# Hybrid decoder layer on one core: block sums on DVE straight from PSUM, norm sums five products later, a third buffer of decays, the gates' tanh as a job

## Chip, cores and metric

One core of a Trainium2 chip runs the whole layer in one launch. The metric is the device time of a launch in microseconds (us), the median of several runs.

## What is computed

One layer of a decoder trunk on 1024 tokens of width 1024, float32. One wide projection feeds three mixers, and their outputs are gated, summed, projected and normalised:

```python
h = rms_norm(x, g_pre)
proj = jnp.einsum('bsd,dc->bsc', h, w_in)
(q, k, v, z_a, u, v_s, z_s, z_m, xbc, dt_raw, gate_logits) = jnp.split(proj, _split_points(), axis=-1)
y_att = sliding_window_attention(q, k, v, sinks, rel_bias) * jax.nn.silu(z_a)
y_sg = chunked_spatial_gate(u, v_s, sg_ln_g, sg_ln_b, sg_w, sg_b) * jax.nn.silu(z_s)
y_ssm = ssd_mixer(z_m, xbc, dt_raw, conv_w, conv_b, dt_bias, a_log, d_skip, ssm_norm_g)
gates = jax.nn.sigmoid(gate_logits.reshape(bsz, seq, N_BRANCHES, D_MODEL))
merged = (gates[:, :, 0] * (y_att @ w_br_att) + gates[:, :, 1] * (y_sg @ w_br_sg)
          + gates[:, :, 2] * (y_ssm @ w_br_ssm))
out = merged @ w_out
return x + rms_norm(out, g_post)
```

`ssd_mixer` (Mamba-2) takes a causal convolution over four tokens and a silu of `xbc`, then scans 8 chunks of 128 tokens in each of 4 groups of 8 heads. A chunk needs the decays `exp(a_cs[l] - a_cs[s])`, a product within the chunk, a product with the carried state, a new state, the skip term, the product with `silu(z)`, and the sum of squares for a norm over the group.

## The kernel before

**Engines and queues.** Each engine works through its own instructions in the order in which they were written, and waits for semaphores of the others: TensorE (PE) for matmuls, VectorE (DVE), ScalarE (ACT) and GpSimd (POOL) for elementwise work, SyncE (SP) for all DMAs. The stage that the change is in has its order written out by hand for all five.

**Products.** That stage computes the projections for xBC, z_m, z_s and u, and most of the gates by a seven-product scheme for 2x2 blocks (Strassen's in Winograd's form). A *unit* is a pair of 128-column tiles of w_in; 39 units make 273 *products*. `PairStream._step` issues one product: it prepares weights up to four products ahead (`_prepare`: POOL block sums in `_sum`, an ACT cast `whi`, and one product later a DVE subtraction `wlo`, L230, in `_second`), then issues 12 matmuls into one of four PSUM banks (three of `ps_mm`, one of `ps_ax`; L290 to L292), and then the sums that make the four output blocks 11, 12, 21 and 22 out of the seven products, in tiles `tp` (8 buffers) and `tu`.

**Block sums before.** Product 0 is copied out by ACT (`s1`, L308), product 1 added by DVE (`u2`, L311). Product 2 is copied out by ACT (`s5`, L313), and POOL adds it to `u2` (`u4`, L314). Product 3 is added by DVE (`u3`, L316), and POOL adds `s5` and `u3` to block 22 (L304). Products 4, 5 and 6 are added by DVE (L302) and end blocks 12, 21 and 11.

**Jobs.** What follows on a block is a generator that is put in `pst.waiting`: a convolution (`conv`: three L781 taps on DVE, a tanh on ACT, L788 on DVE, a store), a silu (`z_pair`, `zu_pair`). `_work`, the last thing that `_step` does, advances two of them by a step, four when the queue is long. A gate's tanh and its store (L725, L727) stand in `gate_pair`'s own `evac`, at once behind the block.

**Chunks.** While products run, the scan of the 32 chunks goes on between them. `chunk(n)` is a generator too; the loop at the end of the stage advances each running chunk by one step ahead of each product, and begins one every 6 products (5 in the last group). In it: the score matmul and the transposes (L873 to L877), two halves of decays (`seg`, filled by a broadcast load; `relu` and an exp on ACT, `local` on DVE, L867), the state product `po` (L912) read by DVE into `t1` (L914), the new state `pn` (L917), the chunk's own product `pd` (L927), added to `y` by DVE (L931), `t1` added by POOL (L933), the product with silu(z) on POOL (L938), its square on ACT (L943), two POOL sums over the square (L945, L946), and, one step behind the sums, a matmul with a column of ones that adds over the partitions (L949). `po`, `pn` and `pd` share two PSUM banks (`ps_a2`), so that `pd` is written where `po` stood.

Ahead of this stage lie attention and the first projections; behind it the spatial gate's mixing (`sg_mix`, between the last products), then the four branch projections and the output.

Of the kernel before, what the change touches and what calls it, by code (L numbers as in the profile page):

```python
# [19 lines left out]
P = 128  # L20
# [19 lines left out]
def hybrid_kernel(ctx, tc, t, out):  # L40
# [153 lines left out]

    class PairStream:
        AHEAD = 4

        def __init__(self, pool, lhs):
            self.pool, self.lhs = pool, lhs
            self.units, self.raw, self.b, self.ops, self.slot = [], {}, {}, {}, None  # L200
            self.prepared = self.done = 0
            self.late = None
            self.waiting, self.active, self.begun = [], [], []
# [57 lines left out]
        def _work(self):  # L261

            for _ in range(2 if len(self.waiting) > 3 else 1):
# [7 lines left out]
        def _step(self):  # L271
# [27 lines left out]
            def block(b, eng, name, x, op=ALU.add):  # L299
                d = t[name][:, 4:]  # L300
                if x is o:
                    eng.tensor_tensor(d, d, o, op=op)  # L302
                else:
                    eng.tensor_tensor(d, x, d, op=op)  # L304
                self.units[u][1](b, t[name])

            if i == 0:
# [4 lines left out]
            elif i == 2:  # L312
                A.copy(tmp("s5"), o)  # L313
                G.tensor_tensor(tmp("u4"), t["u2"], t["s5"][:, 4:], op=ALU.add)  # L314
            elif i == 3:
                V.tensor_tensor(tmp("u3"), t["u2"], o, op=ALU.add)  # L316
                block(22, G, "s5", t["u3"][:, 4:])
            elif i == 4:
                block(12, V, "u4", o)
            elif i == 5:  # L320
                block(21, V, "u3", o, ALU.subtract)
            else:
                block(11, V, "s1", o)
            self._work()
# [412 lines left out]
    def z_pair(g, n):  # L737
# [7 lines left out]
        def evac(b, d):  # L745
            pst.waiting.append(silu(b, d[:, 4:]))
        return [t["w_zm"][2 * g + n][k] for k in range(2)], evac

    def zu_pair(g):
# [11 lines left out]
        def evac(b, d):  # L761
# [4 lines left out]
            else:  # L766
                pst.waiting.append(silu(half, d, us.pop(half)))
        return [t["w_zu"][g][k] for k in range(2)], evac

    def conv_pair(g, n):  # L770
# [23 lines left out]
        def evac(b, d):  # L794
# [7 lines left out]
            pst.waiting += [conv(0, k, d), conv(1, k, d1)]  # L802
# [17 lines left out]
    with tc.tile_pool(name="mp", bufs=1, reuse_waits="tile") as mp, tc.manual_schedule(  # L820
# [18 lines left out]
        def load_a(n):  # L839
            g, c = divmod(n, 8)  # L840
            rows = acs_dr[c * 32 + g * 8:c * 32 + g * 8 + 8, :]
            segs[n] = []
            for i in range(2):
                seg = mp.tile([P, 4, P], F32, name="seg", bufs=2)
                src = rows[i * 4:(i + 1) * 4].rearrange("h l -> (h l)").unsqueeze(0).broadcast_to([P, 4 * P])
                nc.sync.dma_start(out=seg.rearrange("p h l -> p (h l)"), in_=src)
                segs[n].append(seg)
            if c > 0:

                eas[n] = mp.tile([P, 4, P], F32, name="ea")  # L850
                for i in range(2):
                    src = rows.rearrange("(j i) l -> i j l", i=2)[i].unsqueeze(0).broadcast_to([64, 4, P])
                    nc.sync.dma_start(out=eas[n][i * 64:(i + 1) * 64], in_=src)

        def chunk(n):

            g, c = divmod(n, 8)
            seg = segs[n]

            def relu(i):  # L860

                for j in range(4):
                    A.activation(seg[i][:, j, :], seg[i][:, j, :], AF.Relu, scale=-1.0,
                                 bias=acs[:, c, g * 8 + i * 4 + j:g * 8 + i * 4 + j + 1])

            def local(i):
                V.tensor_tensor(seg[i], seg[i], gt.unsqueeze(1).broadcast_to([P, 4, P]), op=ALU.mult)  # L867
# [39 lines left out]
            local(1)  # L907
            if c > 0:
# [4 lines left out]
                t1 = mp.tile([P, 4, P], F32, name="t1")  # L913
                V.scalar_tensor_tensor(t1, v4(po), 0.5, eas.pop(n), op0=ALU.mult, op1=ALU.mult)  # L914
# [10 lines left out]
            for h in range(8):  # L925
                r = slice((h % 2) * 64, (h % 2) * 64 + 64)
                T.matmul(pd[r, (h // 2) * P:(h // 2 + 1) * P], lhsT=xd[:, h * 64:(h + 1) * 64],  # L927
                         rhs=seg[h // 4][:, h % 4, :], start=True, stop=True)
# [5 lines left out]
            if c + 1 < NB:  # L934
                load_a(n + 1)
            yield

            G.tensor_tensor(y, y, zz.pop(n), op=ALU.mult)  # L938
            yield
            if c + 1 < NB:  # L940
                load_z(n + 1)
            sq = mp.tile([P, 4, P], F32, name="t1")
            A.activation(sq, y, AF.Square)  # L943
            yield
            G.tensor_tensor(sq[:, 0:2, :], sq[:, 0:2, :], sq[:, 2:4, :], op=ALU.add)  # L945
            G.tensor_tensor(sq[:, 0, :], sq[:, 0, :], sq[:, 1, :], op=ALU.add)  # L946
# [4 lines left out]
            for j in range(4):  # L951
                A.activation(y[:, j, :], y[:, j, :], AF.Copy, scale=ng[:, g * 4 + j:g * 4 + j + 1])
            if g < 3:
                yield
# [278 lines left out]
```

## Time and profile before

| | |
|---|---|
| median of 3 runs | 1933.63 us (1925.47 to 1934.16) |
| the profiled execution | 1927.05 us, its span 1925.2 us |
| mean granted TensorE clock | 0.966 of full speed |
| the stage with the products | 425 to 1450 us of the span |

The profile is of one execution. Busy time is the time in which an engine executed an instruction; PEld is the load of weights into TensorE. The granted clock of TensorE is 1.00 at 2.4 GHz and 0.50 at 1.2 GHz; a mean between lies over both.

### The profile page before, as it was taken

How to read it: one execution, taken by the hardware profiler on the slowest of the kernel's cores; microseconds unless marked ns; L12 is line 12 of the kernel's file. 1: busy time of each engine (PE TensorE's matmuls, PEld its weight loads, DVE VectorE, ACT ScalarE, POOL GpSimd, SP SyncE). 2: the span in 40 equal slices, each digit the busy share in tenths (PEclk: the TensorE clock that was granted, in tenths of full speed). 3: DMA queues.
4: the chain of work that ended last, by engine and by line, in shares of the span. 5: the costliest groups of instructions: out<-in, count | busy, mean ns of one | idle time of the engine just before them, and what ended most of it. 6: DMA issues, size and time to landing. Idle time of an engine off the chain costs nothing. (4 is left out here: it accounts for less than half of the span.)

```text
span 1925.2 us, 26009 instructions
## 1 busy us (share of the span) xinstructions
PE 1784.2 (93%) x9181; PEld 1493.1 (78%) x9181; DVE 1297.5 (67%) x1815; ACT 838.5 (44%) x1938; POOL 848.9 (44%) x759
## 2 busy tenths in 40 slices
PE   7999999989998889888988998997996999999998
PEld 6988888968886767666866776776884888888898
DVE  6466676578988976898598856776876453535423
ACT  5245555434455565655565556562223120212221
POOL 1026666564546755666565655676545300000000
PEclk9999999989998989999999999998997999999999
DMA  6211111213344544444454444443566453533204
GB/s 222 93 45 44 56 44 56 75 58 94 106 142 135 159 147 129 151 141 137 144 159 121 139 150 143 148 143 116 194 197 242 170 186 98 176 109 109 96 26 154
DMA packets 165378, 243.29 MB, mean 126 GB/s; under 512 B 13152, under 2 KB 105600, under 8 KB 165120
## 3 DMA queue, kind: packets, MB, share of 16 engines
q1 hardware_dynamic: 165248, 241.63, 39.2%
q8 instruction: 73, 1.20, 0.3%
q14 instruction: 57, 0.47, 0.1%
HBM read 177.99 MB, written 63.59 MB: 125 GB/s over the span
## 5 line engine op out<-in xcount | busy, mean ns | idle before, releaser
L115 PE MATMUL ps_mm<-y,whi 128*128 128x512 f32 x512 | 201.9, 394 | 9.8 <-ACT y L1061 9.8
L116 PE MATMUL ps_mm<-y,whi 128*128 128x512 f32 x512 | 202.2, 395 | 7.2 <-DVE y L1062 7.2
L290 PE MATMUL ps_mm<-h,whi 128*128 128x512 f32 x468 | 200.2, 428 | 4.8 <-ACT vst L354 2.8
L117 PE MATMUL ps_mm<-y,wlo 128*128 128x512 f32 x512 | 201.4, 393 | 0.0
L292 PE MATMUL ps_mm<-h,wlo 128*128 128x512 f32 x468 | 188.2, 402 | 5.7 <-DVE wlo L230 5.7
L225 POOL TENSOR_TENSOR ts<-ts,raw 128x512 f32<-128x512 f32 x78 | 124.4, 1594 | 149.0 <-DVE wlo L230 119.3
L291 PE MATMUL ps_mm<-h,whi 128*128 128x512 f32 x468 | 188.6, 403 | 0.0
L97 ACT CAST whi<-raw 128x1024 fp32r<-128x1024 f32 (+1 forms) x69 | 71.6, 1039 | 255.9 <-PE ps_mm L116 227.5
L88 POOL TENSOR_TENSOR rso<-rso,mhalf_row 128x1 f32<-128x1 f32 x8 | 4.4, 554 | 402.3 <-DVE rso L87 402.3
L230 DVE TENSOR_TENSOR wlo<-raw,whi 128x512 fp32r<-128x512 f32 x156 | 158.2, 1015 | 6.9 <-ACT whi L255 6.4
L290 PE MATMUL ps_mm<-S,whi 128*128 128x512 f32 x352 | 148.9, 423 | 0.0
L291 PE MATMUL ps_mm<-S,whi 128*128 128x512 f32 x352 | 141.7, 402 | 0.0
L292 PE MATMUL ps_mm<-S,wlo 128*128 128x512 f32 x352 | 141.3, 401 | 0.0
L781 DVE SCALAR_TENSOR_TENSOR acc<-tp,wcv,acc 128x512 f32<-128x512 f32 x144 | 137.6, 982 | 1.7
L230 DVE TENSOR_TENSOR wlo<-ts,whi 128x512 fp32r<-128x512 f32 x117 | 105.9, 906 | 26.9 <-ACT whi L255 26.8
L1084 DVE SCALAR_TENSOR_TENSOR tm<-gld,ps_mm 128x512 f32<-128x512 f32 x48 | 33.0, 687 | 135.1 <-PE ps_mm L117 135.1
L115 PEld LDWEIGHTS ps_mm<-y,whi 128*128 128x128 f32 x512 | 97.5, 190 | 31.6 <-ACT y L1061 11.1
L115 PE MATMUL ps_mm<-h,whi 128*128 128x512 f32 x304 | 120.9, 398 | 0.1
L116 PEld LDWEIGHTS ps_mm<-y,whi 128*128 128x128 f32 x512 | 97.4, 190 | 30.4 <-DVE y L1062 10.5
L117 PE MATMUL ps_mm<-h,wlo 128*128 128x512 f32 x304 | 118.6, 390 | 0.0
L116 PE MATMUL ps_mm<-h,whi 128*128 128x512 f32 x304 | 118.5, 390 | 0.0
L290 PEld LDWEIGHTS ps_mm<-h,whi 128*128 128x128 f32 x468 | 92.1, 197 | 29.4 <-issue 8.4
(239 smaller groups left out, 4982.2 us busy)
## 6 DMA issues: line engine op xcount, KB each, us to landing
seg<-acs_dr SPq DMA_DIRECT2D x64, 256.0 KB, 3.8
raw<-in_w_br_dram SPq DMA_DIRECT2D x32, 512.0 KB, 4.3
yraw<-y_dr SPq DMA_DIRECT2D x32, 512.0 KB, 4.7
gld<-gate_dr SPq DMA_DIRECT2D x32, 512.0 KB, 3.5
raw<-in_w_xbc_dram SPq DMA_DIRECT2D x24, 512.0 KB, 4.0
raw<-in_w_gp_dram SPq DMA_DIRECT2D x22, 512.0 KB, 3.6
gate_dr<-tp SPq DMA_DIRECT2D x44, 256.0 KB, 2.5
raw<-in_w_zm_dram SPq DMA_DIRECT2D x16, 512.0 KB, 3.5
```

The source lines that it names most:

```text
L88: G.tensor_tensor(dst, dst, mhalf, op=ALU.pow)
L97: A.copy(hi, raw)
L115: T.matmul(ps, lhsT=whi[:, ks], rhs=rhs(0, kt, half), start=kt == 0, stop=False)
L116: T.matmul(ps, lhsT=whi[:, ks], rhs=rhs(1, kt, half), start=False, stop=False)
L117: T.matmul(ps, lhsT=wlo[:, ks], rhs=rhs(0, kt, half), start=False, stop=kt == KT - 1)
L225: G.tensor_tensor(b[out], b[x], b[y], op=op)
L230: V.tensor_tensor(lo, src, hi.bitcast(F32), op=ALU.subtract)
L290: T.matmul(o, lhsT=hi[:, ks], rhs=h0, start=kt == 0, stop=False)
L291: T.matmul(o, lhsT=hi[:, ks], rhs=h1, start=False, stop=False)
L292: T.matmul(o, lhsT=lo[:, ks], rhs=h0, start=False, stop=kt == 3)
L781: V.scalar_tensor_tensor(acc, d[:, 1 + tap:513 + tap], wcv[:, ti, tap:tap + 1], acc, op0=ALU.mult, op1=ALU.add)
L1084: V.scalar_tensor_tensor(tm, gt[0][:, fs], 1.0, ps, op0=ALU.add, op1=ALU.mult)
```

## The change

- **Block sums.** `u4` is made by DVE, by adding product 2 straight from PSUM to `u2`; block 22 (`c22`) is made by DVE, by adding product 3 from PSUM to `u4`. The ACT copy `s5` and both POOL sums are gone. Per unit: one ACT instruction and two POOL instructions less, two DVE instructions more.
- **Order in `_step`.** `_work` stands ahead of the product's block sums, and new jobs go to a list `fresh`, which `_work` takes up one product later. The gates' tanh is such a job.
- **Chunks.** A chunk begins two products later. The first half of its decays is loaded one chunk ahead, with three buffers instead of two, and its relu is issued in the chunk before. `local` comes one product earlier. `t1` takes the place of `ea`, so that the load of the next `ea` waits for POOL's sum. The square goes into the tile of silu(z) and comes one product later, the load of the next silu(z) behind the POOL sums; their result has a tile of its own, `ssy`. The matmul over the partitions comes three products behind the POOL sums, and with the later start five products later than before.
- **Tail.** Two products run between the first `sg_load` and the mixing; jobs left over are finished behind the last product.

```diff
@@ PairStream._work, _step
+            self.waiting, self.fresh = self.waiting + self.fresh, []
...
-            def block(b, eng, name, x, op=ALU.add):
+            def block(b, name, op=ALU.add):
                 d = t[name][:, 4:]
-                if x is o:
-                    eng.tensor_tensor(d, d, o, op=op)
-                else:
-                    eng.tensor_tensor(d, x, d, op=op)
+                V.tensor_tensor(d, d, o, op=op)
                 self.units[u][1](b, t[name])
 
+            self._work()
             if i == 0:
                 A.copy(tmp("s1"), o)
             elif i == 1:
                 t["u2"] = self.pool.tile([P, 512], F32, name="tu", bufs=1)
                 V.tensor_tensor(t["u2"], t["s1"][:, 4:], o, op=ALU.add)
             elif i == 2:
-                A.copy(tmp("s5"), o)
-                G.tensor_tensor(tmp("u4"), t["u2"], t["s5"][:, 4:], op=ALU.add)
+                V.tensor_tensor(tmp("u4"), t["u2"], o, op=ALU.add)
             elif i == 3:
+                V.tensor_tensor(tmp("c22"), t["u4"][:, 4:], o, op=ALU.add)
                 V.tensor_tensor(tmp("u3"), t["u2"], o, op=ALU.add)
-                block(22, G, "s5", t["u3"][:, 4:])
+                self.units[u][1](22, t["c22"])
...
-            self._work()
             return 2.8
@@ gate_pair
-        def evac(b, d):
-            d = d[:, 4:]
+        def tanh(b, d):
             A.activation(d, d, AF.Tanh, scale=0.5)
...
+            yield from ()
+
+        def evac(b, d):
+            pst.fresh.append(tanh(b, d[:, 4:]))
@@ loads and chunk(n)
+        def load_a(n, i):
+            seg = mp.tile([P, 4, P], F32, name="seg", bufs=3)
...
+            A.activation(segs[n, 0], segs[n, 0], AF.Exp, scale=-1.0)
+            if c + 1 < NB:
+                load_a(n + 1, 0)
             yield
...
-            relu(0)
+            local(0)
+            relu(n, 1)
             yield
 
-            A.activation(seg[0], seg[0], AF.Exp, scale=-1.0)
-            relu(1)
-            yield
-
-            local(0)
-            A.activation(seg[1], seg[1], AF.Exp, scale=-1.0)
+            A.activation(segs[n, 1], segs[n, 1], AF.Exp, scale=-1.0)
             if c > 0:
                 A.activation(eas[n], eas[n], AF.Exp)
+            yield
+
+            if c == 0:
+                load_z(n)
+            local(1)
             if g < 3:
                 yield
 
-            local(1)
             if c > 0:
...
-                t1 = mp.tile([P, 4, P], F32, name="t1")
-                V.scalar_tensor_tensor(t1, v4(po), 0.5, eas.pop(n), op0=ALU.mult, op1=ALU.mult)
+                t1 = eas.pop(n)
+                V.scalar_tensor_tensor(t1, v4(po), 0.5, t1, op0=ALU.mult, op1=ALU.mult)
...
             if c + 1 < NB:
-                load_a(n + 1)
+                load_a(n + 1, 1)
+                relu(n + 1, 0)
             yield
 
-            G.tensor_tensor(y, y, zz.pop(n), op=ALU.mult)
+            if c + 1 < NB:
+                load_e(n + 1)
+            sq = zz.pop(n)
+            G.tensor_tensor(y, y, sq, op=ALU.mult)
             yield
+            yield
+            A.activation(sq, y, AF.Square)
...
+            yield
+            ss = mp.tile([P, P], F32, name="ssy")
+            G.tensor_tensor(sq[:, 0:2, :], sq[:, 0:2, :], sq[:, 2:4, :], op=ALU.add)
+            G.tensor_tensor(ss, sq[:, 0, :], sq[:, 1, :], op=ALU.add)
             if c + 1 < NB:
                 load_z(n + 1)
...
             yield
+            nc.sync.dma_start(out=y_dr[g * 4:(g + 1) * 4, :, c * P:(c + 1) * P].rearrange("j p s -> p j s"), in_=y)
+            yield
             yield
             pn = psum(ps_tr, "tr")
-            T.matmul(pn[:, 0:1], lhsT=sq[:, 0, :], rhs=one, start=True, stop=True)
+            T.matmul(pn[:, 0:1], lhsT=ss, rhs=one, start=True, stop=True)
@@ the loop, the mixing, the tail
-                begin[46 + 49 * g + (6 if g < 3 else 5) * c] = g * 8 + c
+                begin[48 + 49 * g + (6 if g < 3 else 5) * c] = g * 8 + c
...
         sg_load(0)
+        pst.run(2)
+        left -= 2
...
     pst.run(4)
+    while pst.fresh or pst.waiting or pst.active:
+        pst._work()
```

What the change moves in the written order is seen at three places. The first is PE at the end of a product, where before the matmul over the partitions (L949) stands alone, ahead of the next product:

```order
L290 MATMUL ps_mm<-S_4294,whi 128x512
L291 MATMUL ps_mm<-S_4295,whi 128x512
L292 MATMUL ps_mm<-S_4294,wlo 128x512
L949 MATMUL ps_tr<-mhalf_row,t_7997 128x1
L290 MATMUL ps_mm<-h_111,whi 128x512
```

Now it is L965, reads `ssy`, and stands ahead of the transposes of a chunk that begins two chunks later:

```order
L294 MATMUL ps_mm<-h_109,wlo 128x512
L965 MATMUL ps_tr<-mhalf_row,ssy 128x1
L876 MATMUL ps_tr<-bcch 128x128
L877 MATMUL ps_tr<-ident,bcch 128x128
L880 MATMUL ps_tr<-ident,xch 128x128 x4
L292 MATMUL ps_mm<-S_4294,whi 128x512
```

The matmul moved; PE's other work stays, with new line numbers. The second place is POOL over the same chunk; before, from the product with silu(z) (L938) to the norm sums (L945, L946), which stand behind two weight sums (L225), the block sums `u4` (L314) and 22 (L304), and the scaling of `xdt` (L892):

```order
L938 TENSOR_TENSOR y<-y,zch 128x512
L225 TENSOR_TENSOR ts<-raw 128x512
L314 TENSOR_TENSOR tp<-tu,tp 128x512
L892 TENSOR_TENSOR xde<-xdt,edec 128x512
L225 TENSOR_TENSOR ts<-ts,raw 128x512
L304 TENSOR_TENSOR tp<-tp 128x512
L945 TENSOR_TENSOR t_7997<-t_7997 128x256
L946 TENSOR_TENSOR t_7997<-t_7997 128x128
```

And now, from the same product (L948) to the sums (L956, L957):

```order
L948 TENSOR_TENSOR y<-y,zch 128x512
L226 TENSOR_TENSOR ts<-raw 128x512
L898 TENSOR_TENSOR xde<-xdt,edec 128x512
L226 TENSOR_TENSOR ts<-ts,raw 128x512
L226 TENSOR_TENSOR raw<-raw 128x512
L956 TENSOR_TENSOR zch<-zch 128x256
L957 TENSOR_TENSOR ssy<-zch 128x128
```

The two block sums went. The third place is DVE around the read of `po` (L914), in a unit whose convolution runs; before, with the taps (L781) behind the block sums (L302) of the product:

```order
L230 TENSOR_TENSOR wlo<-raw,whi 128x512
L302 TENSOR_TENSOR tp<-tp,ps_mm 128x512
L788 SCALAR_TENSOR_TENSOR tp<-tp,acc 128x512 x2
L867 TENSOR_TENSOR seg<-seg,gtm 128x512
L914 SCALAR_TENSOR_TENSOR t_7880<-ps_ac,ea 128x512
L230 TENSOR_TENSOR wlo<-ts,whi 128x512
```

And now, where the read is L920, the silu of a job L744, and the new block sums from PSUM L313 (`u4`) and L315 (block 22):

```order
L231 TENSOR_TENSOR wlo<-raw,whi 128x512
L744 SCALAR_TENSOR_TENSOR tp<-acc,tp 128x512 x2
L311 TENSOR_TENSOR tu<-tp,ps_mm 128x512
L920 SCALAR_TENSOR_TENSOR ea<-ps_ac,ea 128x512
L231 TENSOR_TENSOR wlo<-ts,whi 128x512
L313 TENSOR_TENSOR tp<-tu,ps_ax 128x512
L936 TENSOR_TENSOR st<-st,ps_ac 128x512
L937 TENSOR_TENSOR y<-y,ps_ac 128x512
L231 TENSOR_TENSOR wlo<-raw,whi 128x512
L744 SCALAR_TENSOR_TENSOR tp<-acc,tp 128x512 x2
L315 TENSOR_TENSOR tp<-tp,ps_mm 128x512
L316 TENSOR_TENSOR tp<-tu,ps_mm 128x512
```

A product's job steps stand ahead of its block sum, the second half of the decays no longer stands between the block sum and the read of `po`, and two sums per unit are new.

## Rows read from the trace of the kernel before

**Rows 1.** Busy us of each engine over the span, instructions (the page).

```profile
PE 1784.2 (93%) x9181; PEld 1493.1 (78%) x9181; DVE 1297.5 (67%) x1815; ACT 838.5 (44%) x1938; POOL 848.9 (44%) x759
```

**Rows 2.** Waits of PE: line, waited for, us in total, times, longest.

```profile
PE ps_tr L949 <- POOL t L946: 63.3, 26, 4.1
PE ps_ac L927 <- DVE t L914: 10.7, 6, 2.5
...
PE ps_tr L977 <- POOL ssum L974: 6.5, 1, 6.5
```

**Rows 3.** Stretches: us, busy PE, PEld, DVE, ACT, POOL, then clock, DMA.

```profile
436.00:550.00 114.00, 114.00 (x505) 94.39 (x504) 101.49 (x139) 51.64 (x89) 57.51 (x36) 1.00 0.34 104
425.00:1450.00 1025.00, 931.65 (x4499) 749.81 (x4499) 808.29 (x1080) 531.28 (x1216) 608.92 (x430) 0.95 0.46 143
786.20:984.20 198.00, 175.24 (x858) 139.48 (x858) 159.90 (x214) 114.40 (x271) 120.21 (x86) 0.95 0.46 143
1165.00:1329.00 164.00, 146.39 (x735) 116.20 (x735) 116.15 (x154) 86.18 (x218) 112.75 (x82) 0.94 0.41 130
1329.00:1450.00 121.00, 118.35 (x577) 99.25 (x576) 94.84 (x122) 35.37 (x62) 63.64 (x44) 0.97 0.62 201
813.70:816.90 3.20, 3.20 (x9) 2.53 (x8) 0.00 (x0) 2.71 (x7) 0.07 (x1) 0.50 0.27 82
```

**Rows 4.** Timeline of POOL ahead of one wait of PE: start, us, what.

```profile
803.90 1.74 POOL L314 TENSOR_TENSOR tp<-tu,tp 128x512 f32<-128x512 f32 x1
805.60 1.50 POOL L892 TENSOR_TENSOR xde<-xdt,edec 128x512 f32<-128x512 f32 x1
807.06 1.73 POOL L225 TENSOR_TENSOR ts<-ts,raw 128x512 f32<-128x512 f32 x1
808.75 1.72 POOL L304 TENSOR_TENSOR tp<-tp 128x512 f32<-128x512 f32 x1
810.43 1.24 POOL L945 TENSOR_TENSOR t<-t 128x256 f32<-128x256 f32 x1
811.75 0.78 POOL L946 TENSOR_TENSOR t<-t 128x128 f32<-128x128 f32 x1
```

**Rows 5.** The wait on PE, in the timeline: start, us, [idle before].

```profile
812.59 0.38 PE L949 MATMUL ps_tr<-mhalf_row,t 128*128 128x1 f32 x2 [4.08 <-POOL t L946]
```

**Rows 6.** DVE groups from 786.2 to 984.2: busy us, mean ns, idle before.

```profile
L781 DVE SCALAR_TENSOR_TENSOR acc<-tp,wcv,acc 128x512 f32<-128x512 f32 x36 | 34.9, 996 | 0.4
L230 DVE TENSOR_TENSOR wlo<-raw,whi 128x512 fp32r<-128x512 f32 x28 | 28.0, 1001 | 0.4 <-ACT whi L255 0.3
L230 DVE TENSOR_TENSOR wlo<-ts,whi 128x512 fp32r<-128x512 f32 x21 | 19.6, 933 | 6.1 <-ACT whi L255 6.1
L867 DVE TENSOR_TENSOR seg<-seg,gtm 128x512 f32<-128x512 f32 x16 | 14.2, 889 | 2.1 <-ACT seg L901 1.8 <-ACT seg L896 0.4
L788 DVE SCALAR_TENSOR_TENSOR tp<-tp,acc 128x512 f32<-128x512 f32 x12 | 12.8, 1105 | 0.0
L742 DVE SCALAR_TENSOR_TENSOR tp<-acc,tp 128x512 f32<-128x512 f32 x8 | 10.9, 1397 | 0.0
```

**Rows 7.** Three DVE lines over the run: ns least/median/most, first and last start.

```profile
L302 DVE TENSOR_TENSOR tp<-tp,ps_mm x88: 672/680/690, 445.0 to 1451.4; 128x512 f32<-128x512 f32 x88
...
L781 DVE SCALAR_TENSOR_TENSOR acc<-tp,wcv,acc x144: 737/747/1789, 448.3 to 1103.0; 128x512 f32<-128x512 f32 x144
...
L742 DVE SCALAR_TENSOR_TENSOR tp<-acc,tp x32: 675/942/1792, 473.8 to 1060.8; 128x512 f32<-128x512 f32 x32
```

**Rows 8.** POOL groups from 786.2 to 984.2.

```profile
L304 POOL TENSOR_TENSOR tp<-tp 128x512 f32<-128x512 f32 x7 | 11.5, 1650 | 2.0 <-issue 1.3 <-POOL ts L225 0.7
...
L314 POOL TENSOR_TENSOR tp<-tu,tp 128x512 f32<-128x512 f32 x7 | 10.0, 1435 | 7.4 <-ACT tp L313 7.1 <-ACT ssum L950 0.3
```

**Rows 9.** Waits of DVE from 786.2 to 984.2, the three that are named.

```profile
DVE wlo L230 <- ACT whi L255: 6.4, 4, 4.5
...
DVE seg L867 <- ACT seg L901: 1.8, 2, 1.4
...
DVE seg L867 <- ACT seg L896: 0.4, 1, 0.4
```

More of the change, by code (lines that the diff above doesn't have):

```diff
@@ L202, in __init__ @@
             self.late = None
-            self.waiting, self.active, self.begun = [], [], []
+            self.fresh, self.waiting, self.active, self.begun = [], [], [], []
         def add(self, *units):
@@ L745, in evac @@
         def evac(b, d):
-            pst.waiting.append(silu(b, d[:, 4:]))
+            pst.fresh.append(silu(b, d[:, 4:]))
         return [t["w_zm"][2 * g + n][k] for k in range(2)], evac
@@ L766, in evac @@
             else:
-                pst.waiting.append(silu(half, d, us.pop(half)))
+                pst.fresh.append(silu(half, d, us.pop(half)))
         return [t["w_zu"][g][k] for k in range(2)], evac
@@ L801, in evac @@
             V.tensor_copy(d1[:, 1:4], d[:, 513:516])
-            pst.waiting += [conv(0, k, d), conv(1, k, d1)]
+            pst.fresh += [conv(0, k, d), conv(1, k, d1)]
         return [t["w_xbc"][3 * g + n][k] for k in range(2)], evac
@@ L837, in load_z, with rows @@
             nc.sync.dma_start(out=zz[n], in_=z_dr[n // 8, n % 8])
-        def load_a(n):
+        def rows(n):
             g, c = divmod(n, 8)
-            rows = acs_dr[c * 32 + g * 8:c * 32 + g * 8 + 8, :]
-            segs[n] = []
-            for i in range(2):
[L844 to L853, printed above, removed]
+            return acs_dr[c * 32 + g * 8:c * 32 + g * 8 + 8, :]
@@ new lines, in load_a, with load_e @@
+        def load_a(n, i):
+            seg = mp.tile([P, 4, P], F32, name="seg", bufs=3)
+            src = rows(n)[i * 4:(i + 1) * 4].rearrange("h l -> (h l)").unsqueeze(0).broadcast_to([P, 4 * P])
+            nc.sync.dma_start(out=seg.rearrange("p h l -> p (h l)"), in_=src)
+            segs[n, i] = seg
+        def load_e(n):
+            eas[n] = mp.tile([P, 4, P], F32, name="ea")
+            for i in range(2):
+                src = rows(n).rearrange("(j i) l -> i j l", i=2)[i].unsqueeze(0).broadcast_to([64, 4, P])
+                nc.sync.dma_start(out=eas[n][i * 64:(i + 1) * 64], in_=src)
@@ L855, in chunk, with relu @@
+        def relu(n, i):
+            g, c = divmod(n, 8)
+            seg = segs[n, i]
+            for j in range(4):
+                A.activation(seg[:, j, :], seg[:, j, :], AF.Relu, scale=-1.0,
+                             bias=acs[:, c, g * 8 + i * 4 + j:g * 8 + i * 4 + j + 1])
         def chunk(n):
             g, c = divmod(n, 8)
[L858 to L864, printed above, removed]
@@ L866, in local @@
             def local(i):
-                V.tensor_tensor(seg[i], seg[i], gt.unsqueeze(1).broadcast_to([P, 4, P]), op=ALU.mult)
+                V.tensor_tensor(segs[n, i], segs[n, i], gt.unsqueeze(1).broadcast_to([P, 4, P]), op=ALU.mult)
             x, bc = xs.pop(n), bcs.pop(n)
@@ L927, in chunk @@
                 T.matmul(pd[r, (h // 2) * P:(h // 2 + 1) * P], lhsT=xd[:, h * 64:(h + 1) * 64],
-                         rhs=seg[h // 4][:, h % 4, :], start=True, stop=True)
+                         rhs=segs[n, h // 4][:, h % 4, :], start=True, stop=True)
             if 0 < c < NB - 1:
@@ L959, in hybrid_kernel @@
             for c in range(NB):
-                begin[46 + 49 * g + (6 if g < 3 else 5) * c] = g * 8 + c
+                begin[48 + 49 * g + (6 if g < 3 else 5) * c] = g * 8 + c
         running = []
         while running or begin:
-            if pst.done % 49 == 42 and pst.done // 49 < 4:
-                n = pst.done // 49 * 8
-                load_x(n)
-                load_z(n)
-                load_a(n)
+            w, r = divmod(pst.done, 49)
+            if w < 4 and r == 44:
+                load_x(w * 8)
+                load_a(w * 8, 0)
+            elif w < 4 and r == 46:
+                relu(w * 8, 0)
+            elif w < 4 and r == 47:
+                load_a(w * 8, 1)
             if pst.done in begin:
```

19 lines of the change are left out of this document (6 added, 13 removed).

## Prediction

> **What bounds the kernel now.** The page's busy times come first: PE is busy 93% of the span, DVE 67%, ACT and POOL 44% [rows 1]. These are means over stages, so the stretches come next. From 425 to 1450 us, where the products run, PE is busy 931.65 of 1025 us: 93 us of the span's idle PE time lie here, and the clock is granted at 0.95 [rows 3]. Before the first chunk PE never idles: 114.00 of 114.00 us, at clock 1.00, while DVE is busy 101.49 us, 89% [rows 3]. So DVE at nine tenths does not by itself hold PE up.
>
> The waits say who ends PE's idle time: 63.3 us in 26 waits are L949, the little matmul over the partitions, which waits for POOL's norm sum, the longest 4.1 us; 10.7 us in 6 waits are `pd` (L927), which waits until DVE has read `po` out of the same bank [rows 2]. One place shows why POOL is late. From 803.90 on it works without a gap through six instructions, and the norm sums L945 and L946 are the last; of the 7.9 us from the first start to the start of L946, L314 and L304 took 1.74 and 1.72 [rows 4]. PE stood for 4.08 us, and only then could it begin [rows 5]. Shortly behind the wait, from 813.70 to 816.90, the granted clock is 0.50 with PE busy throughout: a wait costs its length, and then some half-speed work [rows 3].
>
> The scan repeats: one group of eight chunks goes with 49 products, 198.0 us long from 786.2 to 984.2. Of it PE is busy 175.24, DVE 159.90, POOL 120.21, at a mean clock of 0.95 [rows 3]. I cost the change on this period.
>
> **PE's floor in a period.** 198.0 - 175.24 = 22.8 us are idle. A mean clock of 0.95 is 0.10 of the period, 19.8 us, at 1.2 GHz; had PE been busy through all of it, 9.9 us would be regained at 2.4 GHz; since part of it is idle time I take 8. Floor: 198.0 - 22.8 - 8 = 167 us, and it takes every wait gone.
>
> **Norm sums later.** The distance from POOL's sums to the matmul grows from one product to three. 114.00 us hold 505 matmuls, 42 products of 12, so a product is 2.71 us, and the two more give 5.4 us, against 4.1 us for the longest wait. Besides, L314 and L304 leave POOL's queue ahead of the sums, some 3.4 us at the place shown. I take this wait as gone. Below, it could stay where POOL falls further behind; above, no more than 63.3 us and its clock can come from it.
>
> **Block sums on DVE.** Per unit DVE gains two instructions that read PSUM. The nearest row is the same sum in L302, 672 to 690 ns, median 680 [rows 7]: 14 a period are 9.5 us. POOL loses 11.5 + 10.0 = 21.5 us a period [rows 8]. This pays DVE back, for DVE and POOL slow each other: an instruction that reads two operands in SBUF, L742, takes 675 to 1792 ns, while L302 with one operand in PSUM stays within 672 to 690 beside the same POOL [rows 7]. In the period the lengthening is (996-747)x36 + (1001-680)x28 + (933-680)x21 + (889-680)x16 + (1105-680)x12 + (1397-680)x8 ns = 37.5 us, taking the medians of L781 and L302 as the undisturbed times [rows 6, 7]. Over 86 POOL instructions [rows 3] that is 0.44 us each; 14 fewer give back 6.1. The bounds are nothing and all that two-SBUF reads lose in equal share of POOL's busy time, 37.5 x 21.5/120.21 = 6.7. Net, DVE carries 159.90 + 9.5 - 6.1 = 163.3 us a period.
>
> Here a rule of the Trainium skill speaks against the change. Its page Perfetto Trace Analysis, section Optimizing Scalar/DVE Operations, puts a DVE access to PSUM at about 125 ns of overhead against 60 in SBUF. The rows show no such gap: 675 ns is the least with SBUF alone, 672 with PSUM [rows 7]. By the page the 14 sums would cost 0.9 us a period more, an estimate; by the rows nothing, and the measurement decides.
>
> **ACT's part.** The copy L313 goes and the gates' tanh waits in the job queue. ACT is busy 114.40 of 198 us; I cost both at nothing, since DVE and PE cover them. What ACT still holds up on DVE is 6.4 + 1.8 + 0.4 = 8.6 us a period [rows 9]; I leave it in.
>
> **Order of jobs and sums, decays, loads.** With the job steps ahead of the product's block sum, DVE does them while PE still computes. Between the block sum and the read of `po` stood a half of the decays (0.889 us on average [rows 6]) and the job steps of the product; now nothing does. `pd` comes a product (2.71 us) behind `po`, so this wait should mostly go. It returns where taps or a `local` stand late on DVE. A cost hidden in the diff: the load of `ea` now waits on SP for POOL's sum into `y`, that of silu(z) for POOL's norm sums, and behind them in SP's queue stand the loads of weights and the stores of jobs. The loads are needed two to three products later, 5 to 8 us; I cost it at nothing while POOL is on time, and at up to the 4 us of a late POOL, now and then, if not.
>
> **What sets the period then.** PE could do 167. DVE has 163.3 us of work; with its 8.6 us of waiting for ACT, 172. In the stretch before the chunks DVE was 0.89 busy beside a PE that never waited [rows 3]; if that were the most, the period would be 163.3/0.89 = 183. I take 175, between 167 and 183. So DVE becomes a partner in the bound, and of 31 us possible 23 come.
>
> **Sum.** Three groups run at 6 products a chunk from 565 to 1165 us, 600/198 = 3.03 periods: 3.03 x 23 = 70 us (15 x 3.03 = 45 to 31 x 3.03 = 94). The last group, 1165 to 1329: PE idle 164.0 - 146.39 = 17.6, less the 6.5 of L977, which waits for POOL's power behind the last chunk and stays [rows 2]: 11; clock 0.94 is 0.12 x 164 = 20 us at half speed, worth up to 10, I take 6. DVE with six units' sums has 116.15 + 8.2 of about 147 and does not bind: 17 us (8 to 20). In the mixing, 1329 to 1450, the loop ends five products later and leaves DVE 94.84 + 5.4 us in about 121 - 5 x 2.71 = 107; at 0.89 that needs 113: a loss of 3 (0 to 6). In the stretch before the chunks DVE's 101.49 us get six units' sums, 8.2, and lose 12 x 0.44 = 5.3: 104.4 of 114, a loss of 1 (0 to 4). Together 70 + 17 - 3 - 1 = 83 us, 43 to 114 by the bounds.
>
> Against the profiled execution, 1927.05 us, that is 1844. This execution lies 6.6 us under the median of the runs shown, 1933.63, while the lowest run, 1925.47, lies at its side; so I put the median at 1848.
>
> **Rivals.**
> - *PE's floor is reached.* DVE's fill-in during products hides all of its work: gain 110 or more, 1823 and below. For it: the stretch before the chunks, PE unhindered. Against it: there DVE had nothing of a chunk to do between products.
> - *DVE binds harder.* No relief from POOL: 159.90 + 9.5 = 169.4 us of DVE a period, 190 at 0.89; gain 8 a period, 24 + 17 - 4 = 37: 1890; with half the relief about 1875. For it: with every PE wait gone, POOL's instructions fall closer together. Against: the one-PSUM rows that never lengthen. The Trainium skill has a rule for this outcome (Perfetto Trace Analysis, the same section): GpSimd and DVE share a read port, so moving work between those two might not help. The sums here leave that port, by the page SBUF — State Buffer, section Who interferes with whom, where an instruction with at most one SBUF input does not contend; the trace agrees with 690 ns at most.
> - *The wait moves to `pd`: slower.* If at every chunk DVE reads `po` late, PE stands there instead. The read may come 2.71 us behind `po` free of charge. A queue of four lengthened taps ahead of it (4 x 0.996 = 4.0 us) and a sum of 0.68 would make PE wait 2 us; that eats 28 x 2 = 56 of the 83. The point from which it decides is 83/28 = 3.0 us a chunk; at six taps and two sums (7.3 us, a wait of 4.6) it is 128 us lost against 83: about 1970. Against it: longest now 2.5 us, in 6 of 28 chunks [rows 2].
> - *The change does not do what it says.* POOL falls behind by three products too, through the square that ACT makes a product later, and L965 waits as L949 did: gain only the 10.7 and a few: 1920 to 1930.
>
> **How the numbers follow.** The forecast, 1830 to 1866: 0.52. PE's floor, 1813 to 1829: 0.12. DVE binds, 1867 to 1895: 0.18. The change without effect, 1896 to 1943: 0.11, of which 0.05 within half a per cent (1924 to 1943). Slower by the wait at `pd`: 0.07. Faster: 0.52 + 0.12 + 0.18 + 0.06 = 0.88; same 0.05; slower 0.07. The likeliest is 1848. For the range 1815 to 1892 I leave out the slower rival, the one without effect and the last of each edge, about 0.2; half a per cent is what a measurement of this kernel can tell.
>
> **What the next profile would show.** Right: L965 hardly among PE's waits; the period of 49 products near 175 us, at a clock of 0.98 or more; the group of L781 and L742 shorter in the mean, L313 and L315 at 0.68 us; DVE busy 163 us a period, over 90%. Left over: waits of PE for DVE, at L933 or at a product's first matmuls. Wrong: L965 still waiting, or L933 waiting 3 us a chunk, or DVE's two-SBUF groups at 1.0 us as before with DVE near 170, or SP's loads late, seen as PE or POOL waiting for DMA of `raw`, `zch` or `ea`.

## The result and the profile after

The changed kernel takes 1851.41 us (median of 4 runs, 1848.86 to 1853.1) against 1933.89 for the kernel before: 0.9579 of its time, 95% interval 0.9547 to 0.9612. Its profiled execution took 1852.97 us, with a span of 1851.2. The page's busy line, which answers to [rows 1]:

```profile
PE 1755.1 (95%) x9181; PEld 1478.3 (80%) x9181; DVE 1313.7 (71%) x1893; ACT 821.9 (44%) x1899; POOL 748.8 (40%) x681
```

The same 9181 matmuls keep PE busy 29 us less than before, at a mean granted clock of 0.979 instead of 0.966: that is clock. DVE has 78 instructions more and POOL 78 fewer. Waits of PE from 425 to 1450 us, as in [rows 2] (line, waited for, us in total, times, longest):

```profile
PE ps_ac L933 <- DVE ea L920: 28.2, 12, 4.6
...
PE ps_tr L991 <- POOL ssum L988: 7.4, 1, 7.4
...
PE ps_tr L880 <- ACT ssum L966: 1.7, 4, 1.2
```

The norm matmul (L965, before L949) no longer waits; `pd` (L933, before L927) waits 28.2 us instead of 10.7. To compare like with like I cut the product stage at the first matmuls of the 49th, 196th, 237th and 273rd product: three groups of six products a chunk (147 products), the last group (41), the mixing (36).

| us | up to 1st | to 49th | three groups | last group | mixing | rest |
|---|---|---|---|---|---|---|
| before | 421.8 | 141.1 | 591.8 | 162.5 | 130.1 | 477.9 |
| after | 423.3 | 140.7 | 534.8 | 141.8 | 128.9 | 481.7 |

The groups give 57.0 us, the last one 20.7. First before, then after: the windows of the three groups and of the last (us, busy PE, PEld, DVE, ACT, POOL, clock, DMA).

```profile
562.80:1154.60 591.80, 525.61 (x2575) 418.57 (x2575) 477.46 (x636) 338.38 (x801) 359.42 (x258) 0.95 0.46 141
1154.60:1317.10 162.50, 148.20 (x758) 117.55 (x757) 117.89 (x156) 92.95 (x236) 105.90 (x80) 0.96 0.43 138
```

```profile
563.90:1098.70 534.80, 504.82 (x2574) 407.96 (x2573) 480.20 (x681) 334.48 (x793) 304.47 (x214) 0.98 0.55 158
1098.70:1240.50 141.80, 141.74 (x758) 114.61 (x756) 124.26 (x167) 85.94 (x217) 91.86 (x68) 1.00 0.52 154
768.20:946.00 177.80, 167.84 (x859) 135.82 (x858) 159.56 (x228) 111.75 (x264) 102.21 (x72) 0.98 0.54 159
```

In the three groups PE's idle time falls from 66.2 us (591.80 - 525.61) to 30.0, and 20.8 us of busy time go with the clock (0.95 to 0.98): 36.2 + 20.8 = 57.0. In the last group PE does not idle at all. The third row is one period of 49 products, 177.8 us. DVE's groups in it, as in [rows 6]:

```profile
L783 DVE SCALAR_TENSOR_TENSOR acc<-tp,wcv,acc 128x512 f32<-128x512 f32 x36 | 33.4, 954 | 0.4
L231 DVE TENSOR_TENSOR wlo<-raw,whi 128x512 fp32r<-128x512 f32 x28 | 25.0, 894 | 0.0
L231 DVE TENSOR_TENSOR wlo<-ts,whi 128x512 fp32r<-128x512 f32 x21 | 18.2, 864 | 0.6 <-ACT whi L256 0.6
L870 DVE TENSOR_TENSOR seg<-seg,gtm 128x512 f32<-128x512 f32 x16 | 16.0, 1001 | 0.0
L790 DVE SCALAR_TENSOR_TENSOR tp<-tp,acc 128x512 f32<-128x512 f32 x12 | 13.2, 1136 | 0.0
L744 DVE SCALAR_TENSOR_TENSOR tp<-acc,tp 128x512 f32<-128x512 f32 x8 | 8.1, 1056 | 0.0
```

Taps, differences and L744 are shorter, the decays (889 to 1001 ns) and L790 a little longer, and the wait for ACT at `wlo` fell from 6.1 us to 0.6. The new sum L313 over the run (ns least/median/most) is what L302 was in [rows 7]:

```profile
L313 DVE TENSOR_TENSOR tp<-tu,ps_mm x30: 670/676/689, 441.1 to 1359.8; 128x512 f32<-128x512 f32 x30
```

One wait at `pd`: the timeline of DVE, then of PE (start, us, instruction, [idle before]).

```profile
866.29 1.53 DVE L231 TENSOR_TENSOR wlo<-raw,whi 128x512 fp32r<-128x512 f32 x1
867.75 2.98 DVE L783 SCALAR_TENSOR_TENSOR acc<-tp,wcv,acc 128x512 f32<-128x512 f32 x4
870.64 0.68 DVE L303 TENSOR_TENSOR tp<-tp,ps_mm 128x512 f32<-128x512 f32 x1
871.24 0.68 DVE L920 SCALAR_TENSOR_TENSOR ea<-ps_ac,ea 128x512 f32<-128x512 f32 x1
```

```profile
867.32 0.39 PE L293 MATMUL ps_ax<-h,whi 128*128 128x512 f32 x1
867.55 0.39 PE L294 MATMUL ps_ax<-h,wlo 128*128 128x512 f32 x1
871.98 1.09 PE L933 MATMUL ps_ac<-seg,xdt 128*64 128x128 f32 x16 [4.04 <-DVE ea L920]
873.00 0.73 PE L292 MATMUL ps_mm<-h,whi 128*128 128x512 f32 x1
873.53 0.63 PE L293 MATMUL ps_mm<-h,whi 128*128 128x512 f32 x1
873.95 0.63 PE L294 MATMUL ps_mm<-h,wlo 128*128 128x512 f32 x1
```

PE is through with the product behind `po` at 867.9, when DVE has four taps, a block sum and the read still before it. Only L231, with 1.53 us, is slow here: six instructions stand in DVE's program order ahead of the read (L231, four taps, L303), late already. Behind the wait the matmuls start 0.42 us apart instead of 0.23, and the granted clock from 873.0 to 876.5 us is 0.51: half speed.

### The profile page after: what moved, and what is told of

It reads as the page before. It is cut to its first block, busy times and chain, and to the rows that moved or that the text cites. A ratio compares the mean times of both kernels' runs of the same rounds, so it can differ in the third digit from the quotient of the medians.

```text
span 1851.2 us, 25892 instructions
## 1 busy us (share of the span) xinstructions
PE 1755.1 (95%) x9181; PEld 1478.3 (80%) x9181; DVE 1313.7 (71%) x1893; ACT 821.9 (44%) x1899; POOL 748.8 (40%) x681
## 5 line engine op out<-in xcount | busy, mean ns | idle before, releaser
L226 POOL TENSOR_TENSOR ts<-ts,raw 128x512 f32<-128x512 f32 x78 | 138.0, 1769 | 191.8 <-DVE wlo L231 191.6
L292 PE MATMUL ps_mm<-h,whi 128*128 128x512 f32 x468 | 193.7, 414 | 3.2 <-ACT vst L353 2.8
L293 PE MATMUL ps_mm<-h,whi 128*128 128x512 f32 x468 | 184.8, 395 | 0.0
L292 PE MATMUL ps_mm<-S,whi 128*128 128x512 f32 x352 | 147.1, 418 | 0.6 <-DVE tp L303 0.6
L231 DVE TENSOR_TENSOR wlo<-raw,whi 128x512 fp32r<-128x512 f32 x156 | 144.6, 928 | 0.7 <-ACT whi L256 0.6
L293 PE MATMUL ps_mm<-S,whi 128*128 128x512 f32 x352 | 139.3, 396 | 0.0
L783 DVE SCALAR_TENSOR_TENSOR acc<-tp,wcv,acc 128x512 f32<-128x512 f32 x144 | 129.2, 924 | 1.7
L115 PE MATMUL ps_mm<-h,whi 128*128 128x512 f32 x304 | 120.9, 398 | 0.1
L116 PE MATMUL ps_mm<-h,whi 128*128 128x512 f32 x304 | 118.6, 390 | 0.0
L117 PEld LDWEIGHTS ps_mm<-y,wlo 128*128 128x128 f32 x512 | 97.4, 190 | 19.9
L256 ACT CAST whi<-raw 128x512 fp32r<-128x512 f32 x156 | 94.6, 612 | 39.4 <-POOL raw L226 16.3
```

Source lines behind the costliest of these rows:

```text
L115: T.matmul(ps, lhsT=whi[:, ks], rhs=rhs(0, kt, half), start=kt == 0, stop=False)
L116: T.matmul(ps, lhsT=whi[:, ks], rhs=rhs(1, kt, half), start=False, stop=False)
L117: T.matmul(ps, lhsT=wlo[:, ks], rhs=rhs(0, kt, half), start=False, stop=kt == KT - 1)
L226: G.tensor_tensor(b[out], b[x], b[y], op=op)
L231: V.tensor_tensor(lo, src, hi.bitcast(F32), op=ALU.subtract)
L256: A.copy(hi, src)
```

## The experiments

Theory A: the norm wait itself was the cost. Theory B: POOL's load was. Each run's ratio is to runs of the kernel before taken beside it, whose medians lie between 1930.85 and 1933.44 us (1933.89 beside the changed kernel). A difference between two of the times below can hold some 3 us of that spread. All results, with the three groups' length, busy times and clock:

| run | us | ratio to before (95%) | groups | PE | DVE | POOL | clock |
|---|---|---|---|---|---|---|---|
| e1 norm only | 1901.40 | 0.9841 (0.982-0.9862) | 564.3 | 517.2 | 466.6 | 356.1 | 0.95 |
| e2 sums only | 1876.86 | 0.9719 (0.9705-0.9734) | 550.5 | 509.0 | 463.6 | 291.5 | 0.98 |
| e3 no sums | 1886.47 | 0.9765 (0.9748-0.9782) | 560.8 | 513.1 | 492.1 | 369.7 | 0.95 |
| e4 norm near | 1870.65 | 0.9682 (0.9666-0.9698) | 550.3 | 512.4 | 477.2 | 306.4 | 0.96 |
| e5 both | 1868.89 | 0.9665 (0.9645-0.9685) | 539.3 | 505.4 | 462.7 | 290.5 | 0.97 |
| e6 pd later | 1848.77 | 0.9564 (0.9547-0.9582) | 525.8 | 502.2 | 484.4 | 299.9 | 0.98 |
| e7 jobs behind the read | 1841.51 | 0.9521 (0.9506-0.9535) | 523.0 | 501.6 | 483.6 | 302.2 | 0.98 |
| e8 jobs last | 1852.17 | 0.9578 (0.9563-0.9592) | 531.4 | 503.7 | 458.6 | 284.2 | 0.98 |
| e9 e7 and e8 | 1846.97 | 0.9555 (0.9535-0.9574) | 526.0 | 503.6 | 467.7 | 286.4 | 0.98 |
| e10 pd later, norm nearer | 1838.44 | 0.9507 (0.9485-0.9529) | 520.9 | 500.2 | 486.0 | 300.0 | 0.99 |
| e11 tanh at once | 1858.40 | 0.9615 (0.9594-0.9636) | 539.5 | 506.9 | 482.1 | 304.2 | 0.97 |
| e12 e7 and e10 | 1831.14 | 0.9490 (0.9467-0.9514) | 512.2 | 497.4 | 488.1 | 297.5 | 1.00 |

**e1, before, norm matmul two products later.**

```diff
-            G.tensor_tensor(sq[:, 0, :], sq[:, 0, :], sq[:, 1, :], op=ALU.add)
+            ss = mp.tile([P, P], F32, name="ssy")
+            G.tensor_tensor(ss, sq[:, 0, :], sq[:, 1, :], op=ALU.add)
             yield
-            pn = psum(ps_tr, "tr")
-            T.matmul(pn[:, 0:1], lhsT=sq[:, 0, :], rhs=one, start=True, stop=True)
-            A.copy(ssum[:, n:n + 1], pn[:, 0:1])
...
+            if g == 3:
+                yield
+            yield
+            pn = psum(ps_tr, "tr")
+            T.matmul(pn[:, 0:1], lhsT=ss, rhs=one, start=True, stop=True)
+            A.copy(ssum[:, n:n + 1], pn[:, 0:1])
```

> The kernel before with one part of the change: the little matmul over the partitions stands three products behind POOL's norm sums instead of one; block sums, job order and decays as before. Theory A (the norm wait itself was the cost, and POOL was only late by less than two products): the 63.3 us of waits at that matmul go nearly whole, some of it comes back as waits for DVE's read of po, and the time is 1858 to 1882 us. Theory B (POOL's load is the cost: what lets PE run is that the block sums leave POOL): POOL keeps all its work, the wait stays in good part or turns up where PE or DVE wait for another POOL product, and the time is 1905 or more. DVE's two-SBUF groups keep their means of about 1.0 us under both.

The wait at the norm matmul is gone, but only 29.6 us come of it. Neither theory's figure: PE's waits in 425 to 1450 us now begin so.

```profile
PE ps_ac L927 <- DVE t L914: 43.7, 17, 5.5
```

The wait moved to `pd`, 10.7 us to 43.7, and the clock of the groups stays at 0.95. The means of DVE's groups did not all stay: over 560 to 1262 us the taps went from 997 to 1044 ns and L742 from 1398 to 991, with all of POOL's work still there. So a shorter L744 in the changed kernel is no sign of POOL's lighter load by itself.

**e2, before, block sums on DVE.**

```diff
-                A.copy(tmp("s5"), o)
-                G.tensor_tensor(tmp("u4"), t["u2"], t["s5"][:, 4:], op=ALU.add)
+                V.tensor_tensor(tmp("u4"), t["u2"], o, op=ALU.add)
...
-                block(22, G, "s5", t["u3"][:, 4:])
+                self.units[u][1](22, t["c22"])
```

(`c22` is summed ahead of `u3`, as in the change.)

> The kernel before with the other part alone: the block sums u4 and c22 on DVE from PSUM, ACT's copy gone, 14 POOL instructions fewer a period; the norm matmul one product behind POOL's sums as before, job order and decays as before. Theory A: the two POOL instructions ahead of the norm sums (3.4 of 7.9 us at the place shown) go, so the wait at the norm matmul shrinks to 10 to 30 us in all, DVE carries 163 us a period: 1880 to 1905 us. Theory B (POOL's load is the cost): this part alone brings the most of the gain, 1870 or less.

A gain of 54.1 us, beyond theory A's and just short of B's: the larger part alone. The waits are where A put them:

```profile
PE ps_tr L949 <- POOL t L946: 24.8, 16, 3.7
PE ps_ac L927 <- DVE t L914: 16.0, 12, 2.4
```

**e3, changed kernel, block sums as before** (e2's lines the other way round).

> The changed kernel with the block sums back as they were (ACT's copy, two POOL sums per unit), all else changed. Theory A: three products are enough for POOL even with its 21.5 us more a period; DVE loses 9.5 us of sums a period and gets back some 6 of lengthening; the time stays within 10 us of the changed kernel's 1851. Theory B: the norm matmul waits again, or POOL's late operands hold DVE; 1880 or more. DVE's mean for the taps and for the silu products goes back toward 996 and 1397 ns under both.

35 us slower than the changed kernel; theory A said within 10. It is not the norm matmul that waits, which A had right, but again `pd`, and DVE is busy longer with 42 instructions fewer. In the groups its taps go from 954 to 1124 ns, past the 996 that was expected; the silu products hardly move (1179 to 1196). The wait first, then the window of the three groups:

```profile
PE ps_ac L934 <- DVE ea L921: 43.4, 12, 7.2
```

```profile
567.40:1128.20 560.80, 513.14 (x2575) 413.08 (x2573) 492.13 (x639) 347.20 (x819) 369.74 (x257) 0.95 0.54 152
```

**e4, changed kernel, norm matmul one product behind the sums.**

```diff
             nc.sync.dma_start(out=y_dr[g * 4:(g + 1) * 4, :, c * P:(c + 1) * P].rearrange("j p s -> p j s"), in_=y)
-            yield
-            yield
             pn = psum(ps_tr, "tr")
```

> The changed kernel with only the distance undone: the norm matmul stands one product behind POOL's sums again; block sums on DVE, jobs, decays as changed. Theory A: the wait at the norm matmul comes back in part, since POOL now has 102 us of work a period instead of 120 and no block sums ahead of the norm sums: 15 to 35 us of waits, 1866 to 1890. Theory B: POOL is on time with its lighter load, hardly a wait, within 5 us of 1851.

Theory A's band, 19 us lost, with the wait back in part; so the distance counts beside the lighter POOL:

```profile
PE ps_tr L963 <- POOL ssy L957: 22.9, 9, 6.7
```

**e5, before with e1 and e2 together.**

> The kernel before with both parts, the norm matmul two products later and the block sums on DVE, but job order, gates' tanh, decays and loads as before. If the two gains (29.6 and 54.1 us alone) add, 1847; if they overlap, because each takes part of the same waits, 1855 to 1868, and the order of jobs and decays is worth the rest to 1851. Theory C (DVE's lag behind PE is what is left, POOL's instructions lengthen it): waits of PE at L927 of 20 to 40 us stay.

64.6 us of gain, where the two alone give 29.6 + 54.1 = 83.7: they overlap by 19, and the time is 0.9 us above the band for that. What is left stands at `pd`:

```profile
PE ps_ac L927 <- DVE t L914: 33.5, 21, 3.5
```

From here to the changed kernel are 17.5 us, for the order of jobs, the decays and the tanh.

**e6, changed kernel, `pd` one product later in the groups of six.** The sum into `state` stays where it is. Shown are the step that is put in and the one that is left out; the relu of a chunk's second half of decays, the exp of `ea`, and the loads of the next second half and the next `ea` move by a product as well.

```diff
+            if g < 3:
+                if c + 1 < NB:
+                    relu(n + 1, 0)
+                yield
             pd = psum(ps_ac, "ac")
...
             G.tensor_tensor(y, y, sq, op=ALU.mult)
             yield
-            yield
+            if g == 3:
+                yield
```

> The changed kernel with pd a product later in the three groups of six products a chunk, so that two products instead of one lie between the read of po and pd; one half of the decays and the load of ea move by a product with it. Theory D (the wait at pd is one place where the order is too tight, while DVE has 18 us of slack a period elsewhere): the 28.2 us of waits at L933 fall under 6 and their half-speed stretches go: 1815 to 1830. Theory C (DVE is behind PE as a whole, pd is only where that shows): PE waits elsewhere, at a product's first matmuls for a bank or for wlo, and the time stays within 1843 to 1856.

The period falls to 175.3 us (9 us in the three groups of the profiled executions), but the time by 2.6 only, no more than the spread above: theory C's band, though the wait comes at another place than the one that it named. PE's waits show what came in place:

```profile
PE ps_tr L880 <- ACT ssum L978: 13.3, 9, 3.1
PE ps_ac L945 <- DVE ea L925: 10.3, 12, 2.6
```

What `pd` gave up (28.2 to 10.3) stands in good part at the chunk's transposes, which want the bank out of which ACT copies the norm sum.

**e7, changed kernel, the jobs of the product before `po` behind its read.**

```diff
-            self._work()
+            if not self.hold:
+                self._work()
...
             local(1)
             if g < 3:
+                pst.hold = c > 0
                 yield
...
                 V.scalar_tensor_tensor(t1, v4(po), 0.5, t1, op0=ALU.mult, op1=ALU.mult)
+                if g < 3:
+                    pst._work()
+                    pst.hold = False
```

> The changed kernel with the job steps of the one product before po put behind DVE's read of po, in the same three groups; nothing else moves. Theory D: what stands ahead of the read falls by up to two taps or products of silu (1.5 to 3 us), the waits at L933 fall from 28.2 to 8 to 15 us: 1830 to 1842. Theory C: no more than 4 us are gained, 1847 to 1855, as the jobs are then late for pd's sum or the next block sum.

Theory D's time: 9.9 us faster than the changed kernel. The waits at `pd` fall to 17.9 us, not to 8 to 15. At the place shown above DVE reads `po` directly behind the block sum; the four taps come after:

```profile
862.79 0.67 DVE L303 TENSOR_TENSOR tp<-tp,ps_mm 128x512 f32<-128x512 f32 x1
863.39 0.68 DVE L922 SCALAR_TENSOR_TENSOR ea<-ps_ac,ea 128x512 f32<-128x512 f32 x1
863.99 2.97 DVE L784 SCALAR_TENSOR_TENSOR acc<-tp,wcv,acc 128x512 f32<-128x512 f32 x4
```

**e8, changed kernel, job steps behind the block sum again.**

```diff
-            self._work()
             if i == 0:
...
                 block(11, "s1")
+            self._work()
             return 2.8
```

> The changed kernel with the job steps behind the product's block sum again, as before; the gates' tanh stays a job. What stands ahead of the read of po is the same sum of work. Under both theories DVE waits more for products' ends (now 16 us a period) and less work fills them: 1853 to 1866. If the order of jobs and block sums is worth nothing, 1849 to 1853.

No difference (1852.17 against 1851.41): the order of jobs and block sums, taken over all products, is worth nothing in this kernel. Yet DVE's busy time differs by 21.6 us and POOL's by 20.3, in the groups, at the same instructions:

```profile
567.10:1098.50 531.40, 503.69 (x2574) 407.35 (x2573) 458.56 (x680) 331.30 (x783) 284.18 (x214) 0.98 0.56 159
```

**e9, e7 and e8 together.**

> Both orders together: the job steps behind the block sum at every product, and at the product before po (groups of six) behind DVE's read of po as well. With the job steps last DVE's busy time was 1283 us instead of 1314 at the same instructions, for they met less of POOL's work. If what DVE loses beside POOL limits PE, this beats the 1841.5 us of the run with only the one product changed: 1832 to 1838. If that loss falls in time that DVE would stand idle anyway, it stays at 1839 to 1844; if the idle time behind each product counts, it is slower, 1845 or more.

1846.97, slower than e7 by 5.5: the time that DVE saves beside POOL is not what limits PE. A new wait stands at the transposes, for DVE's read of their bank:

```profile
PE ps_tr L881 <- DVE btok L885: 9.7, 6, 2.6
```

**e10, e6 with the norm matmul one product earlier.**

```diff
             yield
-            yield
+            if g == 3:
+                yield
             pn = psum(ps_tr, "tr")
```

> The kernel with pd a product later, and with the norm matmul one product earlier (two behind POOL's sums) in the groups of six, so that its bank is read by ACT before the next chunk's transposes want it. In the run without this, 13.3 us in 9 waits stood at those transposes for ACT's copy of the norm sum, where the changed kernel has 1.7. Theory D (a place that is too tight costs what it waits): those go, no wait comes at the norm matmul, and the time is 1832 to 1840. Theory C (DVE is behind PE as a whole): the 13 us turn up elsewhere and the time stays at 1845 to 1852.

Theory D's band: 10.3 us faster than e6. The groups, where the edit is, give 4.9 us of it (525.8 to 520.9); the rest is not explained. The wait for ACT's copy falls from 13.3 us to 4.1; that at `pd` takes 5.6 of it:

```profile
PE ps_ac L945 <- DVE ea L925: 15.9, 9, 3.8
...
PE ps_tr L880 <- ACT ssum L979: 4.1, 3, 1.4
```

**e11, changed kernel, tanh at once.**

```diff
-            yield from ()
...
-            pst.fresh.append(tanh(b, d[:, 4:]))
+            tanh(b, d[:, 4:])
```

> The changed kernel with the gates' tanh again at once in the block sum's step instead of as a job of the next product. It tells which of the two remaining parts (decays earlier with a third buffer, tanh as a job) brings the 17.5 us between the run with both main parts and the changed kernel. If the decays alone: 1849 to 1854. If the late tanh does: ACT's copies of the weights stand behind the tanh, DVE's waits for ACT at wlo rise from 3.8 toward 16 us, and the time is 1857 to 1868.

7.0 us slower, 4.7 of them in the three groups; DVE's waits for ACT at `wlo` from 560 to 1262 us rise only from 3.8 to 5.4 us. So the late tanh is worth some 5 to 7 us, by another way than the one expected, which this run doesn't name. With the jobs' order at nothing (e8), about 10 of the 17.5 us are left for decays and loads, by subtraction only: no run changes them alone.

**e12, e7 and e10 together.**

> The two changes that helped at pd put together: pd a product later, the norm matmul two behind the sums, and the job steps of the product before po behind DVE's read of po. The one gave 1838.4 us, the other 1841.5 against 1851.4. Theory D (each removes waits at its place): the 15.9 us that stay at pd in the former fall under 6, and the time is 1826 to 1834. Theory C (DVE, 93% busy in the groups of six, has hardly any time left to give): the two overlap, 1835 to 1841, and the waits turn up at another of DVE's operands.

1831.14 us, theory D's band: 20.3 us faster than the changed kernel. The wait at `pd` stays at 8.8 us, not under 6. That wait first, then the window of the groups, at full clock:

```profile
PE ps_ac L950 <- DVE ea L927: 8.8, 6, 1.8
```

```profile
564.90:1077.10 512.20, 497.37 (x2574) 399.45 (x2573) 488.12 (x680) 337.12 (x791) 297.49 (x214) 1.00 0.55 165
```

## Why the prediction came out right, point by point

**The number.** 1848 was forecast and 1851.4 measured, in the likeliest case's own range. By stages it was 70 us for the three groups (57.0 came), 17 for the last (20.7), -3 for the mixing (+1.2), -1 ahead of the chunks (+0.4). The main term was 13 us too large and the three small ones together 9.3 too low; that they make 79.3 against 83 is luck in part. Up to the first product and behind the last, where no term was set, the profiled execution after is 1.5 and 3.8 us longer. Over the kernels here these ends lie at 421.8 to 428.6 and 477.9 to 483.0 us, with the kernel before the lowest in both; whether that is spread or the change is not shown. The profiled spans differ by 74.0 us, the medians by 82.5: the profiled execution before, 1927.05 us, lies near the short end of its runs (1925.47 to 1936.66), and the stages explain only the 74. One sum of the rivals is off: with half the relief, DVE's 166.4 us at 0.89 give about 1880, not 1875.

**Norm sums later.** The wait went, as said; e4 shows that at one product it would be 22.9 us, even with the lighter POOL. What the prediction did not say is that the wait alone buys little: 29.6 us in e1, for PE met the next late link, `pd`, with 43.7 us. The rival "the wait moves to `pd`" was the true mechanism there, short of the size at which it decides.

**Block sums on DVE.** The cost was right: 676 ns against 680. The Trainium skill's larger overhead for PSUM (page Perfetto Trace Analysis, section Optimizing Scalar/DVE Operations) does not show: L313 took 670 to 690 ns, and 675 is the least with SBUF alone [rows 7]. The relief was mis-sized. In the groups 42 sums more on DVE lowered its busy time, from 477.5 to 463.6 (e2), 466.6 to 462.7 (e5 against e1) and 492.1 to 480.2 (changed kernel against e3). Busy time counts the overlap of two records once (above, L303 and L920 start 0.60 us apart and take 0.68 each), so the relief is better taken from the instructions: those of DVE that have nothing in PSUM took 37.0, 27.8 and 36.0 us less in sum in the three pairs. That is 0.88, 0.66 and 0.86 us per sum taken from POOL, where 0.44 was forecast and 0.48 was the upper bound (6.7 us over 14). The even share itself was near. In the trace of the kernel before, every DVE instruction without PSUM that took over 0.78 us ran beside a POOL instruction; sharing what they took beyond 0.68 by the length of overlap puts 22.9 of 113.5 us on L304 and L314, 0.55 us each. In e2 the same count is 77.0 us, so 13.6 came back beside POOL work that stays. The prediction put that at nothing; how much of DVE's work such instructions meet can change by order alone, as e8 shows. The Trainium skill's rule on the same page, that moving work between GpSimd and DVE might not help, is not what came here: the move alone gave 54.1 us. What the Trainium skill says on SBUF — State Buffer, section Who interferes with whom, that an instruction with at most one input in SBUF does not contend, agrees with L313's 670 to 690 ns.

**DVE's work in a period.** 163.3 us forecast, 480.20/3 = 160.1 measured. Two errors nearly cancel, which is luck. Both main parts (e5) lowered it by 4.9 us a period, where 3.4 more were forecast. From there to the changed kernel it rose by 5.8, which was not seen; e8 puts 21.6/3 = 7.2 us down to the jobs' new place.

**Order of jobs: the step that failed.** "This wait should mostly go": it grew from 10.7 to 28.2 us. The growth comes with the end of the wait for the norm sums: in the old order of jobs `pd` waits 43.7 us in e1 and 33.5 in e5. So the new order did not raise it; it failed to remove it. The prediction looked at what stands between the block sum and the read of `po`. But the jobs now stand ahead of the block sum, and the read behind both, so the sum of work ahead of it is what counts; e8, with the jobs behind the block sum, has 24.1 us there. Taking them behind the read (e7) is what helps.

**ACT's part and the decays.** 8.6 us a period of DVE's waits for ACT were left in; at `wlo` 3.8 us remain in all three groups together, and at the decays none. The last group, costed by PE's idle time alone, gave more: 150.2 us in e5, 141.8 after, with PE idle 5.8 and 0.1 us. Decays and loads were not costed there.

**What sets the period.** 175 was forecast, 178.3 is the mean of three. The argument from DVE's 0.89 was wrong as a ceiling: e12 has DVE busy 488.12 of 512.20, 0.95, at 170.7 us a period. What kept the changed kernel above 175 was the wait at `pd`, 28.2/3 = 9.4 us a period and its half-speed work. PE's floor was well placed: 167 forecast, 497.37/3 = 165.8 us busy in e12 at clock 1.00; the term for the clock was 8 and is 525.61/3 - 165.8 = 9.4.

## What to carry to other kernels

Where an engine works in program order, a wait removed is worth its length only until the next late link: run each part alone and both together (29.6, 54.1 and 64.6 us here) before a gain is put down to one of them. For a read that another engine waits for, count all that stands ahead of it in its engine's order since the engine fell behind, not only what is next to it, and move work that nobody waits for behind it. When a place is given more distance, look for what its new neighbours share, such as a bank (e6, e10).

## What was not expected of the hardware

When two POOL sums a unit, of 1.43 and 1.65 us on average [rows 8], left POOL, DVE's other instructions gave back 0.66 to 0.88 us for each, about what the sum costs on DVE itself (0.68) or more. In the kernel before, only some 0.55 us of that lay beside the sums themselves. And DVE's and POOL's busy times can each rise by 20 us in 530 (e8 against the changed kernel) through order alone, with the same instructions and the same time: a busy share of theirs holds time lost to one another, which a kernel can have to spare.
